# Hybrid decoder block: block 0's mixers first, and both of its expert sums beside the chains

## The chip, the cores and the metric

One core of one Trainium2 chip runs the kernel. The metric is the device time of one execution in microseconds (us); smaller is better. Five engines work side by side, each through its own queue in order: TensorE (PE; its weight loads are shown as PEld), VectorE (DVE), ScalarE (ACT), GpSimd (POOL, which here only issues gathers) and SyncE (SP, which issues all other DMAs).

## The reference

512 tokens of 1024 features go through one decoder layer: two mixers that see earlier tokens (A and B), a merge, and a mixture of single-neuron experts (PEER). Cut to what matters:

```python
h = rms_norm(x, norm1_gain)
proj = h @ w_in                               # column groups for both mixers and both merge gates
# A: per query the indexer picks the 128 best causal keys, attention runs over these alone
score = einsum(iw, relu(iq . ik));  _, sel = top_k(score, k_sel);  y_att = softmax(q . k[sel]) @ v[sel]
# B: gated DeltaNet: short conv, SiLU, per chunk of 64 a triangular solve, a state handed on from chunk to chunk
y_dn = rms_norm(gated_deltanet(...), gain) * silu(dz)
merged = sigmoid(ga) * (y_att @ w_att_branch) + sigmoid(gb) * (y_dn @ w_dn_branch)
x = x + merged @ w_o
h2 = rms_norm(x, norm2_gain)
# PEER: 8 heads, 2 x 128 sub-keys each, top 16 of the sums: 128 experts a token out of 16384
q = h2 @ w_query;  s = q . sub_keys;  top_k, top_k;  expert, gate = ...
act = gelu(sum(u_tab[expert] * h2));  x = x + sum((gate * act) * v_tab[expert])
```

## The kernel before, in words

The tokens are four blocks of 128 (block 0 to block 3). Weights come as tiles of 0.5 MB through four buffers (`wt`). What TensorE makes for block 0 alone reads `h0`, what it makes for the other three blocks at once reads `hr`.

Four *chains* run round robin, each a Python generator that yields between dependent steps: two `deltanet` chains (two heads each, block after block), `indexer` (16 rounds of max and replace on VectorE per block) and `attender`. After each step of a chain a *filler* gets turns, 1.6 per step (`FILL_A`) or 1.8 (`FILL_B`). The filler holds what has no chain: `projections(0)` and `projections(1)` (for block 0 and for the rest), and `single(0)` and `single(1)`, each of which takes one block through merge, `w_o`, second norm, query, sub-keys (`path`) and the choice of its 128 experts (`choose`), and ends with writing the indices `eu` (line 902). In the program before, the filler mixes whatever is active: a block's `single` gets two turns for each one of `projections(1)`.

PEER is done in two ways. Blocks 0 and 1 (`SINGLE`) gather: for each of 128 slots, GpSimd issues one indirect DMA that brings a row of 1024 numbers for each of 128 tokens (0.5 MB, `row`), and VectorE sums it: for a u row a product with `h2` and a sum into `act` (line 923), for a v row a multiple added to `x1` (line 934). That makes 4 x 128 = 512 rows, one after another through `all_rows`: before, u of block 0, u of block 1, v of block 0, v of block 1. The gathers go round four buffers (`ROWS`); late in the program eight more are there (`MORE_ROWS`). Blocks 2 and 3 (`WHOLE`) compute all 16384 experts densely: `dense_u(i)` multiplies with a tile `ut` and takes the gelu into `ge`, `spread` writes the chosen gates into a dense matrix (one-hot `oa`, `ob`, products on TensorE, `gb` to DRAM as `gd`), and `dense_v(i)` multiplies `ge` by the gates and sums with `vt` into `acc`.

The stages follow each other: chains and filler until block 1's indices are there; `path(WHOLE)`, with a row at every second step (`STEPS_E`); 36 `dense_u` around the two `choose`, then 16 chunks of `spread`, with four rows a chunk (`CHUNK_ROWS`) and the rest of the first 54 `dense_u`; then 128 `dense_v` with the other 74 `dense_u` and all rows that are left, paced evenly. A scheduler orders the instructions on every engine from this; each engine then keeps that order.

Of the kernel before, what the change touches and what calls it, by code (L numbers as in the profile page):

```python
# [34 lines left out]

FILL_A = 1.6
FILL_B = 1.8
MORE = 6
# [14 lines left out]
ROWS, MORE_ROWS = 4, 8  # L53
STEPS, STEPS_E, CHUNK_ROWS = 2, 2, 4
END = 3
# [30 lines left out]
def tile_block(ctx, tc, x, xT0, xT1, w_in, sc_cols, sc_rows, w_br, w_o, w_q, subT, uT, uv, cst, iota, out, dbg=None):  # L86
# [17 lines left out]
    def load(dst, src):  # L104
        nc.sync.dma_start(dst, src)
# [134 lines left out]
    done = set()  # L240
    rowv = cp.tile([P, 8 + D], F32, name="rowv")
    load(rowv, sc_rows.to_broadcast([P, 8 + D]))
    alog, dtb, n2g = rowv[:, 0:4], rowv[:, 4:8], rowv[:, 8:8 + D]
    io = cp.tile([P, P], F32, name="io")
# [273 lines left out]
    def projections(part):  # L518
        if part == 0:
            for t in ORDER[6:]:  # L520
                yield from conv(t, 0)
            yield from keys(0)
            yield from queries(0)
            yield from output_gates(0)
            return
        for t in ORDER[:6]:
            yield from conv(t, 1)
        yield from scalars(1)
        for t in ORDER[6:]:
            yield from conv(t, 1)  # L530
        for t in range(4):
            S.copy(iqT[:, t, :], (yield from project(CT_IQ + t, 1)))
            if t == 3:
                done.add("index")
            yield
        yield from output_gates(1)
        yield from keys(1)
        yield from queries(1)
        for t in (8 * br + dt for dt in range(8) for br in range(2)):
            o = yield from project(CT_G + t, 1)  # L540
            s_ = tmp()[:, :T - P]
            S.copy(s_, o)
            nc.sync.dma_start(sgd[t], s_)
            yield
# [187 lines left out]

    x1d = {b: dr.tile([P, D], F32, name=f"x1d{b}") for b in (*SINGLE, *WHOLE)}
    uv2 = uv.rearrange("e (t d) -> (e t) d", t=2)
# [4 lines left out]
    def path(bs, place, banks=("mm",)):  # L739
# [38 lines left out]
        for b in bs:  # L778
            x1[b], h2[b] = place("x1", b), place("h2", b)
            load(x1[b], x[col(b), :])  # L780
        hT_ = place("hT", None)

        def second_norm(b):
            r = slice((b - bs[0]) * P, (b - bs[0] + 1) * P)
            nc.sync.dma_start(x1d[b], x1[b])
            s1 = tiny.tile([P, 1], F32, name="s1", bufs=2)
            r2 = tiny.tile([P, 1], F32, name="r2", bufs=2)
            S.activation(h2[b], x1[b], AF.Square, accum_out=s1)
            V.tensor_scalar(s1, s1, 1.0 / D, EPS, op0=ALU.mult, op1=ALU.add)
            rsqrt(r2, s1, "h")  # L790
            V.scalar_tensor_tensor(h2[b], x1[b], r2, n2g, op0=ALU.mult, op1=ALU.mult)
            for half in range(2):
# [61 lines left out]
    def single(b):  # L854
# [3 lines left out]
        def place(name, _):  # L858
            if name in ("m", "hT"):
                return quarter(name)  # L860
            if name == "x1":
                return hp.tile([P, D], F32, name="x1s", tag="hh", bufs=4)
            if name == "h2":
# [43 lines left out]
    rings = [lambda: ep.tile([P, D], F32, name="row", tag="row", bufs=ROWS)]  # L907
    turn_r, emitted = [0], [0]

# [6 lines left out]
    def all_rows():  # L916

        for b in SINGLE:
            while b not in act:
                yield  # L920
            for s in range(P):
# [3 lines left out]
                yield  # L925
        for b in SINGLE:
            for q in range(4):
# [17 lines left out]
    def fill():  # L945

        active, singles, n, b = [projections(0)], list(SINGLE), 0, None
        nexts = [projections(1)]
        while True:
            if b is None and singles and done >= {("y", singles[0], i) for i in range(3)} and (singles[0] == 0 or not nexts and len(active) == 0):  # L950
                b = singles.pop(0)
                active.append(single(b))
            if nexts and len(active) == 0 or nexts and done >= {("z", 0)}:
                active.insert(0, nexts.pop(0))
            if SINGLE[0] in act and n % STEPS == 0:
                rows()
            n += 1
            for g in active + active[1:]:
                if g not in active:
                    continue  # L960
                try:
                    next(g)
                except StopIteration:
                    active.remove(g)
                    if b in act:
                        b = None
                    continue
                yield
            if not active:
                yield  # L970

# [10 lines left out]
    while chains:  # L982
        turn += 1
        for c in chains + (chains[-1:] if MORE and turn % MORE == 0 else []):
# [3 lines left out]
            try:  # L988
# [3 lines left out]
                continue  # L992
            due += FILL_A if ("attention", 1) not in done else FILL_B
            if hop[0]:
# [13 lines left out]
    hT1 = lp.tile([P, 8, NU], F32, name="hT1")  # L1008
    for b in SINGLE:
        x1[b] = lp.tile([P, D], F32, name=f"x1s{b}")  # L1010
        load(x1[b], x1d[b])
    for b in WHOLE:
        sel[b] = [lp.tile([P, 8, 16], F32, name=f"sel{b}{i}") for i in range(2)]
        gate[b] = lp.tile([P, 8, 16], F32, name=f"gate{b}")
# [105 lines left out]
    for b in WHOLE:  # L1120
# [4 lines left out]
        for _ in spread(b, gp):  # L1125
            n += 1
            dense(left * (NCH - n) // NCH)
            rows(CHUNK_ROWS)
    gx.close()
    rx.close()  # L1130
# [128 lines left out]
```

## Time and profile before

| | |
|---|---|
| median of 3 runs | 1865.47 us (1857.95 to 1873.74) |
| the profiled execution | 1860.58 us |
| its span, from the first to the last instruction | 1858.8 us |
| TensorE busy | 1678.5 us, 90% |
| VectorE busy | 1332.8 us, 72% |
| mean granted TensorE clock | 0.95 |

Busy time is the union of an engine's instructions. "Idle before" names what ended an engine's wait. The span and the waits are of the one profiled execution, which is compared with the median only at the end. A matmul on 32-bit numbers has two records in the trace, a transpose one.

### The profile page before, as it was taken

How to read it: one execution, taken by the hardware profiler on the slowest of the kernel's cores; microseconds unless marked ns; L12 is line 12 of the kernel's file. 1: busy time of each engine (PE TensorE's matmuls, PEld its weight loads, DVE VectorE, ACT ScalarE, POOL GpSimd, SP SyncE). 2: the span in 40 equal slices, each digit the busy share in tenths (PEclk: the TensorE clock that was granted, in tenths of full speed). 3: DMA queues.
4: the chain of work that ended last, by engine and by line, in shares of the span. 5: the costliest groups of instructions: out<-in, count | busy, mean ns of one | idle time of the engine just before them, and what ended most of it. 6: DMA issues, size and time to landing. Idle time of an engine off the chain costs nothing.

```text
span 1858.8 us, 24234 instructions
## 1 busy us (share of the span) xinstructions
PE 1678.5 (90%) x8330; PEld 1311.6 (71%) x8330; DVE 1332.8 (72%) x3114; ACT 573.6 (31%) x1165; POOL 629.4 (34%) x516
## 2 busy tenths in 40 slices
PE   6899999899999968895379997699999999999998
PEld 5766686776667766495269996477777777777766
DVE  3733563978678899789996877886865856567675
ACT  5255322221136314011056885011212222122222
POOL 0000000001542443446834435554533533343430
PEclk8999999999998987997779999799999999999999
DMA  5422355343998899999979999999998999999985
GB/s 212 137 102 74 111 193 195 100 142 106 338 328 319 310 361 336 363 343 360 366 271 343 359 366 389 412 409 409 404 373 325 410 354 365 395 365 362 383 312 170
DMA packets 190123, 556.30 MB, mean 299 GB/s; under 512 B 17840, under 2 KB 63664, under 8 KB 187952
## 3 DMA queue, kind: packets, MB, share of 16 engines
q1 hardware_dynamic: 116272, 286.28, 42.4%
q0 software_dynamic: 73728, 268.47, 38.3%
q8 instruction: 66, 1.08, 0.2%
q14 instruction: 57, 0.47, 0.1%
HBM read 528.60 MB, written 25.95 MB: 298 GB/s over the span
## 4 chain that ended last, share of the span: by engine, by line
PE 54%; DVE 15%; issue 12%; DMA 11%; POOL 5%; ACT 2%; DVEq 0%; POOLq 0%; SPq 0%; ACTq 0%
PE acc L94 18%; PE mm L94 14%; DMA row<-in_uv_dram,eu 9%; PE dn L94 5%; POOL row L913 4%; DVE row L923 3%; PE at L94 3%; DVE wk L573 1%; DVE m L572 1%; DMA row__9423<-in_uv_dram,eu 1%; DMA row__8663<-in_uv_dram,eu 1%; DMA row__7536<-in_uv_dram,eu 0%; DMA row__7605<-in_uv_dram,eu 0%; PE at L609 0%; DMA C<-in_cst_dram 0%
## 5 line engine op out<-in xcount | busy, mean ns | idle before, releaser
L913 POOL DMA_INDIRECT row<-in_uv_dram,eu x318 | 386.3, 1215 | 933.0 <-DVE eu L902 455.3
L923 DVE CUSTOM_DVE_ANT_0 row<-row,h 128x1024 f32<-128x1024 f32 x233 | 281.5, 1217 | 59.4 <-DMA row<-in_uv_dram,eu 58.6
L94 PE MATMUL mm<-hT,ut 128*128 128x256 f32 x864 | 204.5, 394 | 64.4 <-ACT ge L1058 34.2
L94 PE MATMUL mm<-hr,wt 128*128 128x384 f32 (+1 forms) x688 | 241.2, 490 | 0.0
L94 PEld LDWEIGHTS mm<-hT,ut 128*128 128x128 f32 x864 | 168.1, 199 | 89.7 <-ACT ge L1058 35.0
L180 DVE TENSOR_TENSOR vl<-vt,vh 128x1024 fp32r<-128x1024 f32 x86 | 104.0, 1220 | 103.9 <-ACT vh L179 103.8
L94 PEld LDWEIGHTS mm<-hr,wt 128*128 128x128 f32 x688 | 122.9, 190 | 75.9 <-issue 8.6
L94 PE MATMUL acc<-vt,ge 128*128 128x512 f32 x336 | 151.0, 592 | 0.0
L94 PE MATMUL acc<-vl,ch 128*128 128x512 f32 x344 | 139.6, 406 | 6.5 <-DVE vl L180 6.5
L94 PE MATMUL acc<-vh,cl 128*128 128x512 f32 x344 | 135.7, 394 | 0.0
L94 PE MATMUL acc<-vh,ch 128*128 128x512 f32 x344 | 121.9, 437 | 3.8 <-ACT gs L1054 3.8
L179 ACT CAST vh<-vt 128x1024 fp32r<-128x1024 f32 x86 | 88.1, 1044 | 85.7 <-DMA vt<-in_uv_dram 85.1
L934 DVE SCALAR_TENSOR_TENSOR x1s<-row,act,x1s 128x1024 f32<-128x1024 f32 x85 | 109.0, 1282 | 3.0 <-DMA row<-in_uv_dram,eu 1.3
L180 DVE TENSOR_TENSOR cl<-gt,ch 128x256 fp32r<-128x256 f32 x86 | 36.3, 423 | 101.2 <-ACT ch L179 97.9
L94 PEld LDWEIGHTS acc<-vt,ge 128*128 128x128 f32 x336 | 63.8, 190 | 62.6 <-issue 60.3
L179 ACT CAST ch<-gt 128x256 fp32r<-128x256 f32 x86 | 34.7, 404 | 231.9 <-PE acc L94 221.8
L94 PE MATMUL mm<-h,wt 128*128 128x128 f32 x624 | 82.4, 291 | 7.2 <-DVE h L202 4.3
L94 PEld LDWEIGHTS mm<-h,wt 128*128 128x128 f32 x624 | 79.3, 206 | 10.8 <-DVE h L202 4.6
L1098 ACT ACTIVATE ob<-ob,sl 128x128 f32<-128x128 f32 x256 | 78.2, 388 | 26.2 <-DVE ob L1095 26.2
L94 PEld LDWEIGHTS acc<-vh,ch 128*128 128x128 f32 x344 | 66.0, 192 | 26.0 <-issue 8.6
L94 PEld LDWEIGHTS acc<-vl,ch 128*128 128x128 f32 x344 | 65.3, 190 | 22.1 <-DVE vl L180 8.2
L94 PE MATMUL mm<-hT,wt 128*128 128x128 f32 x640 | 79.8, 284 | 1.0 <-ACT tmp L849 1.0
(988 smaller groups left out, 3189.8 us busy)
## 6 DMA issues: line engine op xcount, KB each, us to landing
ut<-in_uT_dram SPq DMA_DIRECT2D x128, 512.0 KB
vt<-in_uv_dram SPq DMA_DIRECT2D x128, 512.0 KB
wt<-in_w_in_dram SPq DMA_DIRECT2D x82, 512.0 KB
wt<-in_w_q_dram SPq DMA_DIRECT2D x48, 512.0 KB
gd<-gb SPq DMA_DIRECT2D x16, 1024.0 KB
gt<-gd SPq DMA_DIRECT2D x16, 1024.0 KB
wt<-in_w_br_dram SPq DMA_DIRECT2D x24, 512.0 KB
wt<-in_w_o_dram SPq DMA_DIRECT2D x24, 512.0 KB
```

The costliest lines, as they stand in the source:

```text
L94: hop[0] = PE.matmul(o, l, r, start=start, stop=stop).ins
L179: S.copy(hi, src)
L180: return V.tensor_tensor(lo, src, hi.bitcast(F32), op=ALU.subtract).ins
L572: V.max(m8, src[:, :N])
L573: V.match_replace(wk[:, :N], m8, src[:, :N], TAKEN)
L913: G.indirect_dma_start(out=r, out_offset=None, in_=uv2, in_offset=bass.IndirectOffsetOnAxis(ap=ix, axis=0))
L923: V.tensor_tensor_reduce(r, r, h2[b], 1.0, 0.0, op0=ALU.mult, op1=ALU.add, accum_out=act[b][:, s:s + 1])
L934: V.scalar_tensor_tensor(x1[b], r, act[b][:, s:s + 1], x1[b], op0=ALU.mult, op1=ALU.add)
L1098: S.activation(ob[:, t], ob[:, t], AF.Copy, scale=sl[:, 2, n:n + 1])
```

## The change

Five things are done at once. The filler's turns are 0.9 per chain step until both halves of block 0's DeltaNet are done (`FILL_0`). The filler no longer mixes: `single(b)` has all turns while it is alive, else the first of the projections. Block 0's v rows come right after its u rows, so before block 1's u rows; its `x1` stays in SBUF for that, and is no longer written to DRAM and read back. Rows come at one per two filler turns from block 0's indices on (`PACE`), at every sixth step of `path(WHOLE)` and two per chunk of `spread`; the number of `dense_u` beside `spread` is kept so that eight stay for its end (`LAST_U`). The second norm's gain is loaded into each `h2` tile instead of once for all, and the square's unused output goes to `hT_`.

```diff
-FILL_A = 1.6
-FILL_B = 1.8
+FILL_0, FILL_A, FILL_B = 0.9, 1.6, 1.8
-STEPS, STEPS_E, CHUNK_ROWS = 2, 2, 4
+PACE, STEPS_E, CHUNK_ROWS = 0.5, 6, 2
+LAST_U = 8
...
-    rowv = cp.tile([P, 8 + D], F32, name="rowv")
-    load(rowv, sc_rows.to_broadcast([P, 8 + D]))
-    alog, dtb, n2g = rowv[:, 0:4], rowv[:, 4:8], rowv[:, 8:8 + D]
+    rowv = cp.tile([P, 8], F32, name="rowv")
+    load(rowv, sc_rows[:, 0:8].to_broadcast([P, 8]))
+    alog, dtb = rowv[:, 0:4], rowv[:, 4:8]
...
-        yield from output_gates(1)
         yield from keys(1)
         yield from queries(1)
+        yield from output_gates(1)
...
             load(x1[b], x[col(b), :])
+            load(h2[b], sc_rows[:, 8:8 + D].to_broadcast([P, D]))
...
-            nc.sync.dma_start(x1d[b], x1[b])
+            if b != SINGLE[0]:
+                nc.sync.dma_start(x1d[b], x1[b])
...
-            S.activation(h2[b], x1[b], AF.Square, accum_out=s1)
+            S.activation(hT_[:, :, r], x1[b].rearrange("p (k c) -> p k c", c=P), AF.Square, accum_out=s1)
...
-            V.scalar_tensor_tensor(h2[b], x1[b], r2, n2g, op0=ALU.mult, op1=ALU.mult)
+            V.scalar_tensor_tensor(h2[b], x1[b], r2, h2[b], op0=ALU.mult, op1=ALU.mult)
...
-        for b in SINGLE:
+            while b and not x1_back:
+                yield
             for q in range(4):
...
-        active, singles, n, b = [projections(0)], list(SINGLE), 0, None
-        nexts = [projections(1)]
+        others, singles, alone, b, due = [projections(0), projections(1)], list(SINGLE), None, None, 0.0
         while True:
...
+            ready = singles and done >= {("y", singles[0], i) for i in range(3)}
+            if alone is None and ready and len(others) <= (singles[0] == 0):
                 b = singles.pop(0)
-                active.append(single(b))
...
-            if SINGLE[0] in act and n % STEPS == 0:
-                rows()
+                alone = single(b)
+            if SINGLE[0] in act:
+                due += PACE
+                while due >= 1.0:
+                    due -= 1.0
+                    rows()
+            if alone is not None:
+                if next(alone, True):
+                    alone = None
+            elif others:
+                if next(others[0], True):
+                    others.pop(0)
+            yield
...
-            due += FILL_A if ("attention", 1) not in done else FILL_B
+            due += FILL_0 if ("y", 0, 0) not in done or ("y", 0, 1) not in done else FILL_A if ("attention", 1) not in done else FILL_B
...
-            dense(left * (NCH - n) // NCH)
+            dense(LAST_U + (left - LAST_U) * (NCH - n) // NCH)
             rows(CHUNK_ROWS)
+    dense(0)
```

Three places show what this moves. The first is TensorE's queue while block 0 goes through its query weights (`mm<-hT,wt`) and sub-keys (`mm<-tmp`). Names that begin with `dn` are DeltaNet's, `at` the indexer's and attention's, and `mm<-hr,wt` are projections of the later blocks. Before:

```order
L94 MATMUL mm<-hT,wt 128x128 x16
L94 MATMUL dn_3231<-XX,am 128x128 x2
L330 MATMUL dn_3284<-C,am 128x128 x2
L94 MATMUL mm<-tmp 128x128 x2
L94 MATMUL dn_3264<-XX,s_3262 128x128 x2
L94 MATMUL dn_3264<-s_3262,XX 128x128 x2
L94 MATMUL mm<-hT,wt 128x128 x10
L94 MATMUL at<-colv,tmp 128x2 x3
L94 MATMUL mm<-hT,wt 128x128 x2
L94 MATMUL at<-ikT,iqT 128x512
L94 MATMUL mm<-hT,wt 128x128 x4
L94 MATMUL mm<-hr,wt 128x384 x8
```

And now:

```order
L96 MATMUL mm<-hT,wt 128x128 x16
L96 MATMUL dn_3320<-kT_3273 128x128 x2
L96 MATMUL mm<-tmp 128x128 x2
L96 MATMUL mm<-hT,wt 128x128 x16
L332 MATMUL dn_3427<-C,am 128x128 x2
L96 MATMUL mm<-tmp 128x128 x2
L96 MATMUL mm<-hT,wt 128x128 x16
L96 MATMUL dn_3484<-XX,am 128x128 x2
L96 MATMUL mm<-tmp 128x128 x2
L96 MATMUL mm<-hr,wt 128x387 x8
```

The projections of the later blocks and most of the chains' steps have moved behind block 0's way. Up to block 0's last sub-key product 1,145 matmuls stand before and 888 now: 200 and 72 with `hr`, 312 and 214 of DeltaNet, 89 and 58 of the indexer, attention and norms, and the same 544 others.

The second place is VectorE's queue behind block 0's indices `eu`. A u row's sum is two instructions, `row,act` and `act`. Before:

```order
L902 SCALAR_TENSOR_TENSOR eu_2991<-area 128x128
L923 ISA row,act_2994<-row,h_0_2093 128x1024
L923 ISA act_2994 128x1
...
L417 TENSOR_TENSOR vb<-dn_3729,beta 128x256
L423 TENSOR_TENSOR attT<-dn_3768,dT 128x256
...
L622 TENSOR_TENSOR tmp<-at,sm 128x2x64
L598 ISA t,mx<-at,bias_1918 128x256
```

And now the place where block 0's u rows end and its v rows begin (`x_0`):

```order
L930 ISA row,act_2247<-row,h_0_1715 128x1024
L930 ISA act_2247 128x1
L939 TENSOR_SCALAR eu_2244<-eu_2244 128x128
L414 TENSOR_TENSOR XX<-XX,dn_4526 64x2x64
L575 MATCH_REPLACE wk<-m_3377,wk 128x384
L423 TENSOR_TENSOR eb<-eb,qhT 128x256
...
L942 SCALAR_TENSOR_TENSOR x_0_1714<-row,act_2247,x_0_1714 128x1024
```

Block 0's v rows now stand among the chains' steps, of which more are left behind `eu0`. `eu0` stands behind 845 other instructions of VectorE before, behind 588 now. `eu1` stands behind 111 u rows and 1,286 other instructions before, and behind 128 u rows, 103 v rows and 1,288 others now. From there to the first product of `dense_v` with the gates stand 171 rows before and 60 now (22 of these 111 ahead of the first `oa`), and behind it 230 and 221.

The third place is VectorE's queue in the middle of `spread`. Before:

```order
L1095 TENSOR_TENSOR oa<-io,sl 128x1024
L1095 TENSOR_TENSOR ob<-io,sl 128x1024
L923 ISA row,act_5191<-row,h_1_4401 128x1024
L923 ISA act_5191 128x1
L923 ISA row,act_5191<-row,h_1_4401 128x1024
L923 ISA act_5191 128x1
L923 ISA row,act_5191<-row,h_1_4401 128x1024
L923 ISA act_5191 128x1
```

And now:

```order
L1098 TENSOR_TENSOR oa<-io,sl 128x1024
L1098 TENSOR_TENSOR ob<-io,sl 128x1024
L1098 TENSOR_TENSOR oa<-io,sl 128x1024
L1098 TENSOR_TENSOR ob<-io,sl 128x1024
L1098 TENSOR_TENSOR oa<-io,sl 128x1024
```

No row stands between the one-hot tiles any more.

## Rows read from the trace of the kernel before

**Rows 1.** The page, part 1: span, then busy time of each engine.

```profile
span 1858.8 us, 24234 instructions
PE 1678.5 (90%) x8330; PEld 1311.6 (71%) x8330; DVE 1332.8 (72%) x3114; ACT 573.6 (31%) x1165; POOL 629.4 (34%) x516
```

**Rows 2.** Line 902: durations in ns, then first and last start.

```profile
L902 DVE SCALAR_TENSOR_TENSOR eu<-area x2: 291/292/293, 455.2 to 750.4; 128x128 int32<-128x128 f32 x2
```

**Rows 3.** The dense end's products, same columns.

```profile
L94 PE MATMUL acc<-vh,ch x344: 387/389/799, 1200.9 to 1851.9; 128*128 128x512 f32 x172
```

**Rows 4.** Windows I to IV: length, busy us, granted clock, DMA share, GB/s.

```profile
0.00:455.50 455.50, 419.64 (x2363) 318.57 (x2364) 270.25 (x966) 157.00 (x316) 0.20 (x4) 0.97 0.39 134
455.50:750.70 295.20, 262.22 (x1381) 197.28 (x1380) 237.80 (x736) 91.95 (x183) 123.76 (x115) 0.91 0.92 331
750.70:1200.90 450.20, 353.76 (x2038) 309.65 (x2037) 378.06 (x902) 181.00 (x423) 236.27 (x187) 0.90 0.97 356
1200.90:1858.80 657.90, 642.87 (x2554) 486.08 (x2552) 446.73 (x512) 143.64 (x243) 269.18 (x212) 0.99 0.94 360
```

**Rows 5.** TensorE's waits in III: us in total, times, longest.

```profile
PE mm L94 <- ACT ge L1058: 34.2, 2, 19.6
PE mm L94 <- DMA ut<-in_uT_dram: 30.2, 4, 18.5
PE at L1083 <- DVE bp L687: 13.2, 1, 13.2
PE at L795 <- DVE r L176: 7.3, 1, 7.3
PE at L1083 <- DVE sel L725: 6.9, 1, 6.9
PE dn L94 <- ACT ob L1098: 3.9, 1, 3.9
PE dn L94 <- ACT qt L842: 0.7, 1, 0.7
```

**Rows 6.** Two short windows of III: PE, PEld, DVE, ACT, POOL, clock, DMA.

```profile
850.00:950.00 100.00, 41.05 (x181) 34.51 (x181) 99.28 (x353) 16.82 (x36) 69.86 (x55) 0.71 0.86 320
1150.00:1175.00 25.00, 6.54 (x22) 5.17 (x21) 9.17 (x8) 2.86 (x4) 6.96 (x7) 0.66 1.04 410
```

**Rows 7.** The chain that ended last, inside II: shares by line.

```profile
by line: DMA row<-in_uv_dram,eu 31.2%; DVE row L923 13.6%; issue 11.0%; PE mm L94 7.6%; PE at L94 5.4%; POOL row L913 5.2%; PE dn L94 4.0%; DVE tmp L776 1.3%; PE at L609 1.3%; ACT L767 1.2%; DMA tmp<-sgd 0.9%; DVE t L598 0.9%; DVE oh_s L721
```

**Rows 8.** Block 0's sub-key matmuls between 400 and 470 us.

```profile
L94 PE MATMUL mm<-tmp x8: 275/275/275, 402.7 to 409.8; 128*128 128x128 f32 x8
```

**Rows 9.** Groups by line: count, busy us, mean ns, idle before.

```profile
L94 PE MATMUL mm<-hr,wt 128*128 128x384 f32 (+1 forms) x688 | 241.2, 490 | 0.0
...
L934 DVE SCALAR_TENSOR_TENSOR x1s<-row,act,x1s 128x1024 f32<-128x1024 f32 x85 | 109.0, 1282 | 3.0 <-DMA row<-in_uv_dram,eu 1.3 <-DVE x1s L934 0.2
...
L94 PE MATMUL dn<-XX,s 128*128 128x128 f32 (+1 forms) x192 | 29.9, 277 | 2.6 <-ACT s L395 1.4 <-ACT s L408 1.2
```

**Rows 10.** Window II, instructions of line 923 alone (two to a row).

```profile
455.50:750.70 295.20, 136.15 (x223) 0.91 0.92 331
```

**Rows 11.** Waits of GpSimd and VectorE in II.

```profile
POOL row L913 <- DVE act L923: 82.6, 47, 5.1
DVE row L923 <- DMA row<-in_uv_dram,eu: 42.6, 36, 5.8
```

**Rows 12.** In order of time, the first gathers: start, duration, idle before.

```profile
455.74 1.07 POOL L913 DMA_INDIRECT row<-in_uv_dram,eu  x1 [455.29 <-DVE eu L902]
457.12 0.94 POOL L913 DMA_INDIRECT row<-in_uv_dram,eu  x1 [0.30 <-issue]
...
461.26 1.22 DVE L923 CUSTOM_DVE_ANT_0 row<-row,h 128x1024 f32<-128x1024 f32 x1 [5.80 <-DMA row<-in_uv_dram,eu]
462.41 0.08 DVE L923 DVE_READ_ACCUMULATOR2_ANT act<- 128x1 f32 x1
```

**Rows 13.** ScalarE's waits between 840 and 960 us.

```profile
ACT act L929 <- DVE act L923: 25.5, 1, 25.5
```

More of the change, by code (lines that the diff above doesn't have):

```diff
@@ L730, in choose @@
             nc.sync.dma_start(dbg["gate"][s, :], g_.rearrange("p h k -> p (h k)"))
-    x1d = {b: dr.tile([P, D], F32, name=f"x1d{b}") for b in (*SINGLE, *WHOLE)}
+    x1d = {b: dr.tile([P, D], F32, name=f"x1d{b}") for b in (*SINGLE[1:], *WHOLE)}
     uv2 = uv.rearrange("e (t d) -> (e t) d", t=2)
@@ L861, in place @@
             if name == "x1":
+                if b == SINGLE[0]:
+                    return ep.tile([P, D], F32, name="x1_0")
                 return hp.tile([P, D], F32, name="x1s", tag="hh", bufs=4)
@@ L907, in tile_block @@
     rings = [lambda: ep.tile([P, D], F32, name="row", tag="row", bufs=ROWS)]
-    turn_r, emitted = [0], [0]
+    turn_r, emitted, x1_back = [0], [0], []
     def row_of(ix):
@@ L945, in fill @@
     def fill():
-        active, singles, n, b = [projections(0)], list(SINGLE), 0, None
-        nexts = [projections(1)]
+        others, singles, alone, b, due = [projections(0), projections(1)], list(SINGLE), None, None, 0.0
         while True:
-            if b is None and singles and done >= {("y", singles[0], i) for i in range(3)} and (singles[0] == 0 or not nexts and len(active) == 0):
+            ready = singles and done >= {("y", singles[0], i) for i in range(3)}
+            if alone is None and ready and len(others) <= (singles[0] == 0):
                 b = singles.pop(0)
-                active.append(single(b))
-            if nexts and len(active) == 0 or nexts and done >= {("z", 0)}:
-                active.insert(0, nexts.pop(0))
-            if SINGLE[0] in act and n % STEPS == 0:
-                rows()
[L957 to L970, printed above, removed]
+                alone = single(b)
[11 more added lines that the diff above has]
+            yield
     sgd = [dr.tile([P, T - P], F32, name=f"sgd{t}") for t in range(16)]
@@ L1008, in tile_block @@
     hT1 = lp.tile([P, 8, NU], F32, name="hT1")
-    for b in SINGLE:
+    for b in SINGLE[1:]:
         x1[b] = lp.tile([P, D], F32, name=f"x1s{b}")
         load(x1[b], x1d[b])
+        x1_back.append(b)
     for b in WHOLE:
```

## The prediction

> **What bounds the kernel now.** I read the totals first [rows 1], and then cut the span at three events that the code names. TensorE is busy 90% of the span, so the time is its work plus the stretches in which it stands still; the question is where those lie, and who makes them. The cuts are the expert indices of block 0 and of block 1 (`eu`, line 902, at 455 and 750 us) [rows 2] and the first product of the dense end (`acc`, at 1200.9 us) [rows 3]. I call the stretches I to IV [rows 4].
>
> In IV TensorE stands for 15 of 657.9 us: nothing but its own work bounds it. In III it stands for 450.2 - 353.8 = 96.4 us, and the list of its waits adds up to just that [rows 5]: 34.2 for gelu buffers, 30.2 for `ut` tiles, 20.1 for the choice (13.2 and 6.9, line 1083), 12 for the rest. VectorE is full there: 99.28 of 100 us between 850 and 950 [rows 6]. In II TensorE stands for 33 us, VectorE for 57. The chain inside II shows what paces it [rows 7]: landing gathers 31.2%, row sums 13.6%, issuing gathers 5.2%. Half of the chain is the loop of a row through its four buffers, although only 111 rows are summed there. So rows are not free beside the chains: that is the point on which I forecast.
>
> **The change, stretch by stretch.** The number of rows, weight tiles and matmuls stays; they move. By the order, 111 row sums stand ahead of `eu1` before and 231 after; between `eu1` and the first gate product 171 before and 60 after; behind it 230 and 221.
>
> *I, to `eu0`.* The last sub-key matmul of block 0 ran at 409.8 us [rows 8]; 1,145 matmuls stood ahead of it. Now 888 do: 128 tiles of the later tokens' projections (`hr`) fewer, at 241.2/344 = 0.70 us each (two records a matmul) [rows 9], 90 us; and 129 small ones of the chains fewer, at 29.9/96 = 0.31 us [rows 9], 40 us. TensorE was busy 419.6 of 455.5 us, so the work taken away is time: 409.8 - 130 = 280. The choice took 455.2 - 409.8 = 45 us beside other VectorE work, of which less is left: 40. `eu0` comes at **320**, 135 us sooner.
>
> *II, `eu0` to `eu1`.* Up to `eu1` VectorE did 270.3 + 237.8 = 508.1 us of work [rows 4], of which rows 136.2 [rows 10], 1.23 each: 371.9 of other work, by 1,286 instructions. Now 588 of these stand ahead of `eu0`, at the mean 170 us; 202 us are left for II. To these come 128 row sums of u at 1.23 (157 us) and, new here, 103 of v at 1.28 (132 us) [rows 9]. That is **491 us of VectorE work in one queue, in order, against 237.8 before**. No cover exists for it: `eu1`'s own choice stands behind the rows in that queue. To the work come waits. VectorE stood 42.6 us for gathers over 111 rows [rows 11], 0.38 a row, and 15 us for all else. The upper bound is 231 x 0.38 + 15 = 104 us. The lower is one filling of the ring, 5.8 us [rows 12], if all other gathers come in time behind other work. Rows stand 2.1 us apart in the order on average (491/231), a little closer than they ran in II (295.2/111 = 2.7), and a gather takes 455.74 to 461.26, or 5.5 us, before a buffer can be summed [rows 12], so with 1.3 for its sum and 0.3 until the next issue four buffers give a row every 1.8 us at best. That lies close to the spacing, so I stay nearer the upper end: 65. II lasts 556 and `eu1` comes at **876**, 125 us later than now. TensorE has 419.6 + 262.2 - 290 = 392 us of work for these 556; it will stand for some 160, and its granted clock, 0.91 in II, will fall further, which costs nothing while VectorE is last. DMA moved 331 GB/s in II, 97.7 MB; 120 more rows of 0.52 MB and 16 more weight tiles make 169 MB, 304 GB/s over 556 us: it is not the tighter bound, but it forbids less than 169/356 = 475 us at the rate of III.
>
> *III.* 111 rows leave, 111 x 1.23 = 137 us of VectorE's 378.1. TensorE's 353.8 us stay. Of its waits, one gelu wait of 19.6 us goes for sure: ScalarE stood at block 0's own gelu (line 929), 25.5 us for the last row of u [rows 13], and that is now in II. The `ut` waits, the longest 18.5 us at 1150 to 1175, where DMA ran at 410 GB/s [rows 6], go with the rows beside the spread; the eight `dense_u` kept for its end fill what the landing gates leave open. The choice stays: it is a chain on VectorE, but with 22 rows less ahead of it (27 us) it costs perhaps 12 of its 20. Bounds for what is left: 12 us (the rest alone) and 76 (only the sure one gone); I take 30, since VectorE's relief is larger than all waits together. III lasts **384**, 66 us less.
>
> *IV.* 221 instead of 230 rows, under TensorE's work: 658, as now.
>
> *The small edits.* Four loads of the norm's gain, 0.5 MB each, replace one; the write and reading back of block 0's `x1` go (1 MB). That is some 0.5 MB more, on SP's queue beside 169 MB: nothing. The square's output goes to another tile, at the same size: nothing. Reordered projections (output gates last) move no work.
>
> Sum: 320 + 556 + 384 + 658 = 1918, and the 1.8 us that lie around the span (1860.6 - 1858.8): **1920**. The profiled execution took 1860.6, 4.9 under the median of 1865.5; I compare with the former for the sum. A measurement of this kernel can tell about 1% from no change.
>
> **A rule that speaks against the change.** A gather's issue lasted 123.76/115 = 1.08 us in II, and 69.86/55 = 1.27 where VectorE was full [rows 4, 6]. This agrees with the Trainium skill, "SBUF — State Buffer", section "SBUF: two separate sides": GpSimd writes the descriptors of its DMAs through a port that some VectorE instructions lock, so a full VectorE starves gathers. By the rule each turn of the four-slot ring is 0.19 us longer, 231/4 turns, 11 us, and the sum 1931.
>
> **Rivals.**
> *Faster: the rows slip in between.* If gathers nearly always land behind other VectorE work, II costs 491 + 5 and III keeps 12 us of waits: 315 + 496 + 366 + 658 + 2 = **1837**. For it speaks that VectorE ran at 99.28% among rows from 850 on [rows 6]; against it that eight more buffers stood there, and that II waited for 36 gathers with more room between them [rows 11]. It decides where VectorE's idle time in II and TensorE's in III together stay under some 25 us. The Trainium skill, "DMA: Bandwidth & Descriptors", section "Anatomy of one DMA — SWDGE (gpsimd) path", gives 2.0 us and the bytes at 436 GB/s, by which an estimate for a gather is 3.2 us and this rival would hold; the trace's 5.5 us disagrees.
> *About even: half of it.* Waits of 20 in II and 20 in III: 320 + 511 + 374 + 658 + 2 = **1865**.
> *Slower still: each row waits as now, and III is not freed.* 104 in II and 76 in III: 320 + 595 + 430 + 658 + 2 = **2005**; half of that excess, 1960, is what I think possible.
> *It doesn't do what it says.* If the scheduler kept rows between the spread's steps, III would keep its `ut` waits: 25 us more, 1945. The order shows no row there, so I give it little.
>
> **How the numbers follow.** The forecast has 0.55 with its neighbours from 1884 to 1950; the faster rival 0.13 (all below 1847); the even case 0.17 (1847 to 1884); the two slow ones 0.15. Likeliest 1920. The range leaves out the faster rival's core and the far slow end: 1858 to 1972. Faster by over 1%: 0.13; within: 0.17; slower: 0.70.
>
> **What the profile after would show.** `eu0` near 320 and the first gather right behind it: if it comes past 350, step I is wrong. `eu1` near 876, with VectorE busy about 490 us between the two and TensorE at some 70%: if `eu1` stands before 830, the waits for rows were overrated, and the result is even or faster. The stretch from `eu1` to the first `acc` near 384, with `ut` waits gone. The dense end within 10 us of 658. The prediction falls if II is short because VectorE's other work lies elsewhere than the order's mean says, or if III's waits were not VectorE's doing.

## The result, and the profile after

The changed kernel takes 1928.31 us (median of 4 runs, 1920.08 to 1935.84), the kernel before 1868.86 beside it: a ratio of 1.0326, 95% interval 1.0258 to 1.0393. It is slower, by 8 us more than the 1920 that was forecast. Its profiled execution took 1924.78 us, of which the span is 1923.0.

The page, part 1, and the events at which the span is cut, of the changed kernel; they answer to [rows 1 to 3, 8]:

```profile
span 1923.0 us, 24217 instructions
PE 1707.5 (89%) x8330; PEld 1320.9 (69%) x8330; DVE 1323.2 (69%) x3114; ACT 566.1 (29%) x1160; POOL 605.3 (31%) x516
...
L96 PE MATMUL mm<-tmp x32: 275/275/377, 252.4 to 286.3; 128*128 128x128 f32 x32
...
L909 DVE SCALAR_TENSOR_TENSOR eu<-area x2: 291/293/295, 317.2 to 860.3; 128x128 int32<-128x128 f32 x2
...
L96 PE MATMUL acc<-vh,ch x344: 387/393/799, 1272.4 to 1916.2; 128*128 128x512 f32 x172
```

Windows I to IV of the changed kernel, columns as in [rows 4]:

```profile
0.00:317.50 317.50, 285.33 (x1805) 235.62 (x1806) 168.92 (x663) 116.28 (x234) 0.20 (x4) 0.96 0.49 166
317.50:860.60 543.10, 428.41 (x1942) 295.75 (x1942) 477.92 (x1180) 126.97 (x261) 252.02 (x234) 0.86 0.89 313
860.60:1272.40 411.80, 361.90 (x2097) 318.39 (x2095) 234.54 (x655) 178.18 (x422) 78.29 (x69) 0.95 0.74 254
1272.40:1923.00 650.60, 631.90 (x2488) 471.13 (x2488) 441.81 (x620) 144.69 (x244) 274.83 (x209) 0.99 0.92 353
```

Beside [rows 4], I is 138 us shorter, II 247.9 longer, III 38.4 and IV 7.3 shorter: 64.2 us in all. The work on VectorE is the same (1323 against 1333 us). TensorE is busy 29 us longer with as many matmuls (its granted clock in II is 0.86 beside 0.91), and stands 215.5 us instead of 180.3.

VectorE's waits in II, which answer to [rows 11], then TensorE's in II, then TensorE's in III, which answer to [rows 5]:

```profile
DVE row L930 <- DMA row<-in_uv_dram,eu: 33.5, 38, 2.8
DVE x L942 <- DMA row<-in_uv_dram,eu: 23.8, 24, 2.8
...
PE dn L332 <- DVE ot L459: 41.0, 2, 37.3
PE dn L96 <- DVE XX L401: 12.0, 10, 2.9
PE at L96 <- ACT R L563: 11.5, 1, 11.5
...
PE mm L96 <- ACT ge L1061: 19.5, 2, 18.8
PE at L1086 <- DVE sel L727: 11.9, 2, 6.9
PE at L800 <- DVE rs_t L177: 5.5, 1, 5.5
```

Waits for gathers in II are 57 us; with 8 us for all else they make the 65 that were forecast. In III the `ut` waits [rows 5] are down to 0.7 us, and a gelu wait of 18.8 us stays. New is a stand of TensorE for one DeltaNet step, 37.3 us long. It is the thread that the experiments follow.

### The profile page after: what moved, and what is told of

Read it like the earlier page. It is cut to its first block, busy times and chain, and to the rows that moved or that the text cites. A ratio compares the mean times of both kernels' runs of the same rounds, so it can differ in the third digit from the quotient of the medians.

```text
span 1923.0 us, 24217 instructions
## 1 busy us (share of the span) xinstructions
PE 1707.5 (89%) x8330; PEld 1320.9 (69%) x8330; DVE 1323.2 (69%) x3114; ACT 566.1 (29%) x1160; POOL 605.3 (31%) x516
## 3 DMA queue, kind: packets, MB, share of 16 engines
q8 instruction: 66, 1.08, 0.2%
## 4 chain that ended last, share of the span: by engine, by line
PE 38%; DVE 9%; issue 9%; DMA 7%; POOL 4%; ACT 1%; SPq 0%; DVEq 0%; POOLq 0%; ACTq 0%
PE acc L96 11%; PE mm L96 11%; PE dn L96 5%; DMA row<-in_uv_dram,eu 3%; POOL row L920 2%; PE at L96 2%; DVE x L942 1%; DMA gt<-gd 1%; DMA wt<-in_w_br_dram 1%; DVE row L930 1%; DMA ut<-in_uT_dram 1%; DVE ti L657 0%; DMA gd<-gb 0%; DVE sr L655 0%; DVE ti L654 0%
## 5 line engine op out<-in xcount | busy, mean ns | idle before, releaser
L96 PE MATMUL mm<-hr,wt 128*128 128x384 f32 (+1 forms) x688 | 248.6, 506 | 0.5 <-issue 0.5
L930 DVE CUSTOM_DVE_ANT_0 row<-row,h 128x1024 f32<-128x1024 f32 x173 | 210.5, 1219 | 33.9 <-DMA row<-in_uv_dram,eu 33.5
L96 PE MATMUL mm<-hT,ut 128*128 128x256 f32 x864 | 198.9, 387 | 23.3 <-ACT ge L1061 19.5
L96 PEld LDWEIGHTS mm<-hr,wt 128*128 128x128 f32 x688 | 128.0, 196 | 92.7 <-issue 24.3
L942 DVE SCALAR_TENSOR_TENSOR x<-row,act,x 128x1024 f32<-128x1024 f32 x128 | 163.7, 1279 | 34.8 <-DMA row<-in_uv_dram,eu 34.0
L1098 DVE TENSOR_TENSOR oa<-io,sl 128x1024 f32<-128x1024 f32 x32 | 39.1, 1223 | 138.2 <-PE dn L96 138.2
L96 PE MATMUL acc<-vh,ch 128*128 128x512 f32 x344 | 115.5, 434 | 7.2 <-ACT ch L181 5.3
L182 DVE TENSOR_TENSOR cl<-gt,ch 128x256 fp32r<-128x256 f32 x86 | 36.3, 423 | 105.9 <-ACT ch L181 103.3
```

The lines of the kernel that those rows point to most:

```text
L96: hop[0] = PE.matmul(o, l, r, start=start, stop=stop).ins
L182: return V.tensor_tensor(lo, src, hi.bitcast(F32), op=ALU.subtract).ins
L930: V.tensor_tensor_reduce(r, r, h2[b], 1.0, 0.0, op0=ALU.mult, op1=ALU.add, accum_out=act[b][:, s:s + 1])
L942: V.scalar_tensor_tensor(x1[b], r, act[b][:, s:s + 1], x1[b], op0=ALU.mult, op1=ALU.add)
L1098: V.tensor_tensor(o_, io[:, None].to_broadcast([P, TB, P]), which, op=ALU.is_equal)
```

## The experiments

The first table gives what each kernel is; rows are counted in the order of VectorE's queue ahead of `eu1`, from there to the first gate product, and behind it. Stages are those of the profiled execution, in us, cut to within 0.4. Medians are of the timed runs; the three kernels without an interval had one execution each.

| kernel | rows | I | II | III | IV | median, ratio [95%] |
|---|---|---|---|---|---|---|
| before | 111, 171, 230 | 455.5 | 295.2 | 450.2 | 657.9 | 1863 to 1869 |
| changed | 231, 60, 221 | 317.5 | 543.1 | 411.8 | 650.6 | 1928.31, 1.033 [1.026, 1.039] |
| half row pace | 142, 32, 338 | 319.2 | 478.1 | 432.2 | 774.3 | 2001.27, 1.074 [1.071, 1.077] |
| half row pace, 6 a chunk | 142, 96, 274 | 317.5 | 479.9 | 456.6 | 691.0 | 1940.68, 1.042 [1.040, 1.044] |
| narrow gather | 249, 42, 221 | 320.3 | 518.0 | 378.9 | 627.6 | 1846.62 |
| routing as before | 231, 141, 140 | 319.7 | 545.0 | 446.7 | 640.4 | 1953.5, 1.049 [1.047, 1.051] |
| turns alone | 222, 63, 227 | 320.1 | 530.4 | 444.0 | 664.6 | 1962.02, 1.054 [1.050, 1.059] |
| turns undone | 110, 153, 249 | 453.9 | 286.7 | 443.4 | 679.7 | 1870.68, 1.005 [1.002, 1.007] |
| even pace | 144, 147, 221 | 393.8 | 364.5 | 433.3 | 649.0 | 1841.57, 0.988 [0.984, 0.993] |
| before, new routing | 111, 94, 307 | 457.4 | 296.5 | 440.7 | 725.3 | 1912.03, 1.026 [1.021, 1.030] |
| pace 1.25 | 222, 70, 220 | 346.7 | 521.0 | 428.3 | 655.1 | 1953.44, 1.047 [1.043, 1.051] |
| pace alone | 128, 163, 221 | 355.4 | 444.5 | 455.6 | 667.3 | 1932.88, 1.036 [1.033, 1.040] |
| no early rows, 0.9 | 36, 21, 455 | 318.3 | 364.8 | 435.4 | 906.2 | 2026.44 |
| no early rows, 1.6 | 36, 21, 455 | 393.6 | 301.9 | 428.1 | 907.3 | 2032.72 |

### Are the rows late by their transfer, or by VectorE's queue?

The narrow gather fetches 64 columns a row, and the sum reads them 16 times, so that VectorE's work is the same and the bytes are a sixteenth; the experts' values are left out.

```diff
-    rings = [lambda: ep.tile([P, D], F32, name="row", tag="row", bufs=ROWS)]
+    rings = [lambda: ep.tile([P, 64], F32, name="row", tag="row", bufs=ROWS)]
...
-                V.tensor_tensor_reduce(r, r, h2[b], 1.0, 0.0, op0=ALU.mult, op1=ALU.add, accum_out=act[b][:, s:s + 1])
+                V.tensor_tensor_reduce(in16(junk), wide(r), in16(h2[b]), 1.0, 0.0, op0=ALU.mult, op1=ALU.add, accum_out=act[b][:, s:s + 1])
```

> The changed kernel, but each gather brings 64 columns in place of 1024, from other places of the table, and the sums run over 1024 columns by reading these 64 sixteen times; it leaves out the values of the experts, the numbers of instructions stay. 249 rows stand ahead of eu1. Theory (VectorE's queue): VectorE's work in II is 189 + 249 x 1.25 = 500 us, its waits for rows go, II lasts about 508 us. Rival (the ring of gathers and DMA's rate pace II): II falls to TensorE's 428 us and little more, about 440.

Window II of the narrow gather, columns as above:

```profile
320.30:838.30 518.00, 438.75 (x1988) 298.95 (x1987) 495.44 (x1204) 130.44 (x264) 298.08 (x252) 0.88 0.37 114
```

II fell by 25 us only, with DMA at 114 GB/s instead of 313: VectorE is busy 495 of 518 us. The transfers are not what makes II long; 18 more rows slipped into it. The ring and the DMA as the cause fall.

### Fewer rows ahead of the second indices

Two kernels: half the row pace with the changed kernel's two rows a chunk of `spread`, and with six.

```diff
-PACE, STEPS_E, CHUNK_ROWS = 0.5, 6, 2
+PACE, STEPS_E, CHUNK_ROWS = 0.25, 6, 2
...
-PACE, STEPS_E, CHUNK_ROWS = 0.5, 6, 2
+PACE, STEPS_E, CHUNK_ROWS = 0.25, 6, 6
```

> The changed kernel with PACE 0.25 in place of 0.5: by the order 142 rows stand ahead of eu1 (231 in the changed kernel), 32 between eu1 and the first gate product, 338 behind it. Theory (II is VectorE's queue, its rows and its waits for them): VectorE's work in II falls to 189 + 142 x 1.25 = 367 us, TensorE's 428 us is last, II falls from 543 to about 470 and eu1 comes near 787. III stays near 405. The rows go into IV, which moves 230 MB in 651 us; 117 more rows make 291 MB, at 405 GB/s 719 us, so IV becomes 720 and the whole 1914. Rival (the turns' order, which leaves the later blocks' projections and chains for II, and not the rows, makes II long): II stays over 520, the whole near 1970. Second rival (IV has room under TensorE's work): IV stays at 655, the whole near 1850.

> The changed kernel with PACE 0.25 and six rows a chunk of the spread in place of two: 142 rows ahead of eu1, 96 up to the first gate product, 274 behind it. Theory: II 470 as with half the pace, III 425 (VectorE 314 of it), IV 655 (258 MB), the whole 1869, as the kernel before. Rival (turns' order): II over 520, the whole 1920 or more.

Both took far longer than expected: II missed by 8 to 10 us, but IV took 774.3 instead of 720 and 691.0 instead of 655, and with six rows a chunk III took 456.6 instead of 425.

89 rows fewer ahead of `eu1` bring it 63 us forward, 0.7 us a row, where a row's sum alone is 1.22 to 1.28. And `eu1` comes at 797 with 142 rows ahead of it, where before it came at 750 with 111. VectorE was busy 369 of II's 478 us, so its queue was not full; TensorE stood 36.3 us for the same `ot`. That was the first sign that something besides the number of rows costs. The other finding is in IV: 338 rows there made 774.3 us. TensorE's wait in IV, of the half row pace:

```profile
PE acc L96 <- DVE vl L182: 93.3, 19, 10.5
```

The dense end needs VectorE for splitting its weights (`vl`), and row sums stand ahead of these. By the table, IV takes 640 us with 140 rows, 649 to 667 with 220 to 230, 680 with 249, 691 with 274, 725 with 307, 774 with 338 and 906 with 455: up to some 220 rows cost little, beyond that about 1.1 us each on the mean ((906.2 - 650.6)/234, from the changed kernel to no early rows at 0.9).

### The routing part

The changed kernel with the old routing, and the old kernel with the new routing (`STEPS_E`, `CHUNK_ROWS`, `LAST_U`).

```diff
-PACE, STEPS_E, CHUNK_ROWS = 0.5, 6, 2
+PACE, STEPS_E, CHUNK_ROWS = 0.5, 2, 4
...
-            dense(LAST_U + (left - LAST_U) * (NCH - n) // NCH)
+            dense(left * (NCH - n) // NCH)
```

And in the kernel before:

```diff
-STEPS, STEPS_E, CHUNK_ROWS = 2, 2, 4
+STEPS, STEPS_E, CHUNK_ROWS = 2, 6, 2
+LAST_U = 8
...
-            dense(left * (NCH - n) // NCH)
+            dense(LAST_U + (left - LAST_U) * (NCH - n) // NCH)
...
+    dense(0)
```

> The changed kernel with the routing part undone (a row at every second step of the path, four rows a chunk, no dense_u kept for the end): I and II stay as in the changed kernel, 317 and 543 us. Theory (rows beside the routing delay what TensorE waits for): 81 rows more in III, 100 us of VectorE's time, III goes from 412 to about 440 us; IV, bound by TensorE, stays at 645 with 140 rows; the whole is 1947, 1% over the changed kernel. Rival (III is bound by TensorE's work, rows there are free): III stays at 415 and the whole at 1920.

> The kernel before with the routing part of the change alone: a row at every sixth step of the last blocks' path, two a chunk of spread, eight dense products kept for its end. Rows 111 ahead of the second indices, 94 from there to the first gate product, 307 behind. Indices as before (455, 750). If rows beside the routing are what stretches it, the third stage falls from 450 to 400 or so, and the dense end, by the runs with 274 (691) and 338 rows (774) in it, rises from 658 to 730: 1885. If the waits there were not VectorE's doing, the third stage stays at 450 and the whole takes 1930.

In the changed kernel the new routing is worth 35 us of III and gives 10 back in IV, near what was expected. In the old kernel it saves 9.5 us of III and costs 67 in IV, because 307 rows are left for it: 1912.03 instead of the 1885 expected. So in these two kernels fewer rows beside the routing pay only where the rows were summed before it.

### Turns, pace of turns, or rows?

Three kernels undo one part of the change each. *Turns alone* keeps the turns and emits as many rows at each stage as the old kernel, with its routing:

```diff
-PACE, STEPS_E, CHUNK_ROWS = 0.5, 6, 2
+PACE, STEPS_E, CHUNK_ROWS = 0.316, 2, 4
...
-            dense(LAST_U + (left - LAST_U) * (NCH - n) // NCH)
+            dense(left * (NCH - n) // NCH)
```

*Turns undone* has the old mixing filler, the old order of projections and 1.6 turns, with the new order of rows and as many of them emitted at each stage as in the changed kernel:

```diff
-FILL_0, FILL_A, FILL_B = 0.9, 1.6, 1.8
+FILL_0, FILL_A, FILL_B = 1.6, 1.6, 1.8
-PACE, STEPS_E, CHUNK_ROWS = 0.5, 6, 2
+PACE, STEPS_E, CHUNK_ROWS = .79, 6, 2
...
-                alone = single(b)
+                active.append(single(b))
...
-            if alone is not None:
-                if next(alone, True):
-                    alone = None
...
+            for g in active + active[1:]:
```

*Even pace* undoes `FILL_0` alone, with a row pace that keeps the count of emitted rows:

```diff
-FILL_0, FILL_A, FILL_B = 0.9, 1.6, 1.8
+FILL_0, FILL_A, FILL_B = 1.6, 1.6, 1.8
-PACE, STEPS_E, CHUNK_ROWS = 0.5, 6, 2
+PACE, STEPS_E, CHUNK_ROWS = 0.655, 6, 2
```

> The changed kernel's turns, chain pace and order of row sums, but as many rows at each stage as before: PACE 0.316, a row at every second step of the last blocks' path, four a chunk of spread, no dense products kept for its end. 285 rows stand ahead of the first gate product (before 282, changed 291), 227 behind. If the cost is the rows' work in VectorE's queue, this kernel has no more of it than the one before: first gate product near 1205, dense end 655, 1865 in all. If the order of turns itself costs (at half the pace the gate product came at 1229 with only 174 rows ahead of it, 28 us later than before with 282), it comes at 1290 to 1310, and the whole takes 1945 to 1965.

> The changed kernel with the old mixing filler, the old pace of turns (1.6) and the old order of projections, but the new row order (block 0's v behind its u), the new routing and a row pace that emits as many rows as the changed kernel at each stage (233, 258 and 290 by the end of chains, path and spread). The scheduler sets 110 rows ahead of the second indices, 153 from there to the first gate product, 249 behind. If the order of turns is what costs, this is as fast as the kernel before or faster: 750 to the second indices, gate product 1175 to 1200, dense end 665, 1845 to 1865. If the row order and row pace cost, the gate product comes near 1270 as in the changed kernel, and the whole takes 1930.

> The changed kernel with 1.6 turns per chain step from the start (FILL_0 undone) and PACE 0.655, so that again 234, 259 and 291 rows are emitted by the end of chains, path and spread. By the order 778 other instructions of VectorE stand ahead of the first indices instead of 588, 144 rows ahead of the second ones, 147 from there to the first gate product, 221 behind. If the loss lies in the chains' being hurried first and TensorE's later standing idle for them, block 0's indices come at 390 to 420, the gate product at 1210 to 1230, the whole takes 1870 to 1890. If it lies in the filler's turns by block alone or in the rows, it stays at 1920 to 1935.

Turns alone is slower than the changed kernel, with the old kernel's count of rows ahead of the gate products (285 against 282). Turns undone equals the kernel before within half a per cent (1870.68 us, a little over the 1845 to 1865 that were expected). And the even pace, with all else of the change but its row pace, is faster than the kernels before and after: 1841.57 us, 0.988 of the kernel before, and faster than the 1870 to 1890 that were expected. It comes to the gate products at 1191.6 us where the changed kernel comes at 1272.4, with 291 rows ahead of them in both. Its windows:

```profile
0.00:393.80 393.80, 365.57 (x2199) 287.34 (x2200) 241.97 (x883) 140.43 (x291) 0.20 (x4) 0.98 0.42 145
393.80:758.30 364.50, 321.88 (x1533) 233.79 (x1532) 302.00 (x870) 101.72 (x204) 157.49 (x147) 0.88 0.91 327
758.30:1191.60 433.30, 355.18 (x2050) 311.35 (x2048) 351.28 (x767) 178.39 (x418) 204.24 (x163) 0.90 0.96 345
1191.60:1840.60 649.00, 637.99 (x2554) 481.69 (x2552) 432.22 (x600) 145.27 (x247) 257.66 (x203) 1.00 0.92 356
```

I loses 76 us to the changed kernel and II wins 179 back. But the scheduler also sets 144 rows ahead of `eu1` here, not 231, and in the other two 222 and 110, so the pace and the rows ahead of `eu1` had to be told apart.

### The pace by itself, with rows and without

*Pace alone* is the kernel before with `FILL_0 = 0.9` and nothing else:

```diff
-            due += FILL_A if ("attention", 1) not in done else FILL_B
+            due += FILL_0 if ("y", 0, 0) not in done or ("y", 0, 1) not in done else FILL_A if ("attention", 1) not in done else FILL_B
```

*Pace 1.25* stands between 0.9 and 1.6, and the two kernels without early rows have `PACE` 0, one at 0.9 turns, one at 1.6:

```diff
-FILL_0, FILL_A, FILL_B = 0.9, 1.6, 1.8
+FILL_0, FILL_A, FILL_B = 1.25, 1.6, 1.8
-PACE, STEPS_E, CHUNK_ROWS = 0.5, 6, 2
+PACE, STEPS_E, CHUNK_ROWS = 0.56, 6, 2
...
-PACE, STEPS_E, CHUNK_ROWS = 0.5, 6, 2
+PACE, STEPS_E, CHUNK_ROWS = 0.0, 6, 2
```

> The kernel before with one edit, 0.9 turns per chain step until both halves of block 0's DeltaNet are done. By the order 626 other instructions of VectorE stand ahead of the first indices (before 846), 128 rows ahead of the second ones (111), 163 from there to the gate product (171), 221 behind (230). If rows ahead of the second indices make the loss, it is 17 rows, some 20 to 25 us: second indices near 773, 1885 in all. If the hurried chains make it by themselves, some 40 us come on top: second indices at 790 to 815, gate product 1240 to 1260, 1915 to 1930.

> The changed kernel with 1.25 turns per chain step at first, half way between its 0.9 and the even 1.6, and PACE 0.56, so that again 292 rows stand ahead of the first gate product. The scheduler sets 663 other instructions of VectorE ahead of the first indices, and 222 rows ahead of the second ones: nearly as many as in the changed kernel (231), where the even pace has 144. If the rows ahead of the second indices make the loss, these come at 840 to 860, the gate product at 1255 to 1275, and the whole takes 1910 to 1925. If the hurried chains themselves make it, half of the difference goes: second indices near 805, gate product near 1230, 1880 in all.

> The changed kernel with PACE 0: no row before the last blocks' path, so 455 rows fall into the dense end and the total time means nothing; 36 rows stand ahead of the second indices by the order. It prices the hurried chains without rows, by the time of the second indices, against its twin at 1.6 turns. If only rows cost, the second indices come in both within 10 us of each other, at 700 to 720, where TensorE's own work (675 to 690 up to there) ends. If the hurried chains cost by themselves, they come 30 to 45 us later here than there.

> The twin of the run without early rows, with 1.6 turns per chain step from the start: 36 rows ahead of the second indices. Second indices at 700 to 720 in either theory; what counts is the difference to the twin. Beside the run at the same pace with 144 rows ahead of the second indices (758), it also gives what such rows cost there: 40 to 58 us for 108 rows if some of them slip into VectorE's idle time, 160 if each costs its full 1.25 us and its wait.

The single edit of the pace makes the old kernel 3.6% slower, as slow as the whole change, with only 17 more rows ahead of `eu1`. In that kernel the number of rows there is not the cause, then. Nor is the hurry by itself: without early rows `eu1` comes at 683 us at 0.9 turns and at 695 at 1.6 (one execution each), so that the hurry gains 12, where a loss of 30 to 45 was expected if it cost by itself. Only both together lose. Rows ahead of `eu1` cost 63 us for 108 at 1.6 turns (695 to 758) and 114 us for 106 at 0.9 (683 to 797): with nearly the same rows ahead of it, `eu1` comes 39 us later at the hurried pace. VectorE's waits in II show where these 39 us are, first of the half row pace (142 rows, 0.9 turns), with its window, then of the even pace (144 rows, 1.6 turns):

```profile
319.20:797.30 478.10, 388.71 (x1824) 267.34 (x1823) 369.29 (x1077) 125.92 (x258) 158.25 (x147) 0.87 0.73 250
DVE row L930 <- DMA row<-in_uv_dram,eu: 39.4, 42, 3.2
DVE t L600 <- PE at L96: 13.1, 10, 3.4
DVE lists L653 <- ACT tmp L854: 12.4, 6, 4.0
```

```profile
DVE row L930 <- DMA row<-in_uv_dram,eu: 43.9, 38, 4.7
DVE XX L401 <- PE dn L96: 3.8, 3, 1.5
DVE t L600 <- PE at L96: 3.6, 4, 1.2
```

Waits for gathers are alike in the two, 43 and 45 us. But VectorE stands 66 us for all else, nearly all of it TensorE's and ScalarE's results, at the half row pace, and 17 at the even pace. With 128 rows and 0.9 turns (pace alone) it stands about 60 us for all else. With 231 rows (the changed kernel) it stands 8: its queue is full, and nothing that TensorE is late with holds it up.

Pace 1.25 points the same way. It has 222 rows ahead of `eu1`, which comes at 867 us, no earlier than in the changed kernel (860). It was expected at 840 to 860 if rows ahead of `eu1` cost, and near 805 if the hurry does; so for kernels with that many rows this run speaks for the rows. It took 1953 us in all, where 1910 to 1925 and 1880 were expected; why it is slower than the changed kernel stays open. No kernel here has 1.6 turns and some 230 rows ahead of `eu1`.

Where rows and hurry meet is seen in windows of 50 us (TensorE's busy time is the second number), of the changed kernel, then without early rows at 0.9, then at the even pace:

```profile
400.00:450.00 50.00, 26.36 (x138) 18.22 (x138) 45.11 (x116) 7.37 (x17) 27.98 (x25) 0.80 0.84 286
450.00:500.00 50.00, 22.77 (x62) 12.26 (x63) 43.36 (x124) 9.24 (x21) 28.94 (x26) 0.62 0.81 275
```

```profile
400.00:450.00 50.00, 49.24 (x192) 28.98 (x191) 24.02 (x79) 13.32 (x32) 0.00 (x0) 1.00 0.30 96
450.00:500.00 50.00, 50.00 (x180) 28.36 (x178) 34.14 (x107) 12.77 (x29) 0.00 (x0) 1.00 0.29 92
```

```profile
400.00:450.00 50.00, 42.43 (x179) 28.94 (x177) 43.48 (x99) 8.37 (x20) 27.25 (x23) 0.86 0.85 293
450.00:500.00 50.00, 48.04 (x164) 28.40 (x165) 44.39 (x127) 12.76 (x30) 22.86 (x23) 0.93 0.93 329
```

VectorE is as busy at the changed and at the even pace (88 us), and the gathers nearly (57 and 50 us of issuing); TensorE does 49 us of work in the one and 90 in the other. The timeline of the changed kernel in that hole: first TensorE, then VectorE's queue meanwhile (start, duration, idle before in brackets).

```profile
430.17 0.39 PE L96 MATMUL dn<-vn,attT 128*128 128x128 f32 x2
467.81 0.66 PE L332 MATMUL dn<-C,ot 128*128 128x128 f32 x2 [37.25 <-DVE ot L459]
...
438.07 1.21 DVE L930 CUSTOM_DVE_ANT_0 row<-row,h 128x1024 f32<-128x1024 f32 x1
439.21 0.08 DVE L930 DVE_READ_ACCUMULATOR2_ANT act<- 128x1 f32 x1
439.21 0.16 DVE L173 TENSOR_SCALAR rs_t<-s 128x2 int32<-128x2 int32 x1
440.03 1.22 DVE L930 CUSTOM_DVE_ANT_0 row<-row,h 128x1024 f32<-128x1024 f32 x1 [0.66 <-DMA row<-in_uv_dram,eu]
441.18 0.08 DVE L930 DVE_READ_ACCUMULATOR2_ANT act<- 128x1 f32 x1
441.18 0.16 DVE L173 TENSOR_SCALAR rs_t<-s 128x2 int32<-128x2 int32 x1
441.25 0.42 DVE L574 MAX8 m<-wk 128x8 f32<-128x256 f32 x1
441.59 0.15 DVE L174 TENSOR_SCALAR r<-rs_t 128x2 int32<-128x2 int32 x1
```

The norm of a DeltaNet output is a chain of small steps on 2 numbers a partition (`rs_t`, `r`, `rs_a`), 0.15 us each, and ahead of nearly every one stands a row sum of 1.22 us, with the wait for its gather. The norm's first and last steps (ScalarE's square of `ot`, VectorE's product `ot`; minimum, median and maximum in ns, then first and last start) of the changed kernel, without early rows at 0.9, and at the even pace:

```profile
L339 ACT ACTIVATE s<-ot x2: 417/417/417, 429.7 to 431.0; 128x256 f32<-128x256 f32 x2
L459 DVE TENSOR_TENSOR ot<-ot,r x2: 420/445/470, 467.2 to 467.6; 128x256 f32<-128x256 f32 x2
```

```profile
L339 ACT ACTIVATE s<-ot x1: 417/417/417, 465.5 to 465.5; 128x256 f32<-128x256 f32 x1
L459 DVE TENSOR_TENSOR ot<-ot,r x1: 408/408/408, 475.3 to 475.3; 128x256 f32<-128x256 f32 x1
```

```profile
L339 ACT ACTIVATE s<-ot x2: 416/416/417, 444.5 to 448.9; 128x256 f32<-128x256 f32 x2
L459 DVE TENSOR_TENSOR ot<-ot,r x2: 406/412/418, 483.5 to 486.9; 128x256 f32<-128x256 f32 x2
```

Without rows the norm takes 9.8 us; with rows it takes 37 at the hurried pace, and 38 to 39 at the even one as well. The even pace pays next to nothing for it, because of what TensorE's queue holds between (its groups from 449 to 487 us at the even pace):

```profile
L96 PE MATMUL mm<-hr,wt 128*128 128x384 f32 x80 | 30.1, 527 | 0.0
```

Eighty records, or forty products, of the later blocks' projections stand between the output and its transposes, and TensorE is busy 35.0 of these 38 us. In the changed kernel none stands there: the transposes follow the output directly, and everything behind them waits, projections too. That these products make the difference is read from the two traces; no run moves them alone. The half row pace has the same stand (36.3 us). In pace alone TensorE stands 26.3 us at the same place, right behind the output, but for a step of the indexer (`R`), for which ScalarE in its turn waited 24.9 us for VectorE.

## Why the prediction came out, point by point

The sum is nearer than its terms. The four stretches missed by -2.5, -13, +28 and -7 us, which leave 5; so close a sum is luck.

**I** was forecast at 320 and took 317.5. The last sub-key product came at 286.3, not 280, and the choice behind it took 31 us, not 40. The prediction gives the whole gain to what no longer stands ahead in TensorE's queue, and does not say which edit makes it: of the 138 us, the even pace has 62 with 1.6 turns, and the 0.9 turns bring the other 76.

**II** was forecast at 556 and took 543.1, with 478 us of VectorE work (491 forecast) and 57 us of waits for gathers and 8 of others (65 forecast). TensorE stood 115 us, not 160. The terms are right in size, and the waits stayed nearer the upper end, as chosen. The narrow gather confirms that VectorE, not the transfers, paced the rows. For this kernel the mechanism holds too: VectorE works or waits for a row in 535 of the 543 us, so that TensorE's standing, the 37.3 us included, "costs nothing while VectorE is last". What the prediction did not see is what lies under it. With fewer rows ahead of `eu1`, VectorE is no longer last, and at 0.9 turns TensorE's stands then come back to it as waits: pace alone is as slow with 128 rows and VectorE busy 340 of 444.5 us. What the rows do there is stretch the chain's small steps nearly four times over; what that costs depends on whether TensorE's queue holds other work at those places, and `FILL_0` took it away. So `FILL_0` gains 76 us in I, and it alone makes the old kernel 3.6% slower. With 1.6 turns and a row pace to match, the rest of the change is 1.2% faster than the kernel before. How the changed kernel's own loss divides between its 231 rows ahead of `eu1` and the 0.9 turns is not shown.

**III** was forecast at 384 and took 411.8; this is the term that was mis-sized. TensorE's work was 361.9 instead of 353.8 us, and its waits were 49.9 instead of 30. The `ut` waits and 8 of the choice's 20 us went as forecast; a gelu wait such as the one that was to go "for sure" was there again. It stands at 981 to 1000 us, and ScalarE was then waiting 22.6 us for VectorE's gates of the choice, with the gelus queued behind:

```profile
ACT gate L692 <- DVE gate L691: 22.6, 1, 22.6
...
999.96 5.26 PE L96 MATMUL mm<-hT,ut 128*128 128x256 f32 x16 [18.79 <-ACT ge L1061]
```

**IV** was forecast at 658 and took 650.6, with 221 rows; the table's slope beyond 221 rows shows that this stage was near its edge.

The **rival that it doesn't do what it says** is out: no row stands between the spread's steps, and the `ut` waits are down to 0.7 us. The **faster rival**, that gathers nearly always land behind other work, is out too: VectorE waited 57 us for them, not 5. So is the **even case**, with 20 us of waits in II and 20 in III: they were 65 and 50. The **slower rival**, each row at its upper price, did not occur.

The **rule on the shared port** (the Trainium skill, "SBUF — State Buffer", section "SBUF: two separate sides") would make a gather's issue longer where VectorE holds the port, by the prediction where VectorE is full. From stage to stage the issue does not follow VectorE's share: in II of the changed kernel VectorE was busy 88%, and an issue took 252.02/234 = 1.08 us, as in II before; in IV, with VectorE at 68%, it took 274.83/209 = 1.31. So the 11 us did not appear. Within a stage the trace agrees with the rule's direction: in II the 25 issues during which VectorE was idle for over half of the time took 0.95 us on the mean and the other 209 took 1.09; in IV 29 took 0.98 and 180 took 1.37. What makes the rest of the difference between the stages stays open.

## What to carry to other kernels

Work that is put "beside" a chain of small dependent steps on the same in-order engine stretches every link by its own length: 1.2-us sums between 0.15-us steps made a 10-us norm last 38. Ask then first whether that engine is full: if it is, each piece of work costs its own length, as here with 231 rows. If it is not, ask what the engine that waits for the chain's end has in its queue meanwhile: with independent products spread over the whole chain TensorE worked 35 of the same 38 us, and with the chain hurried ahead of them it stood for 37. A stage that is bound by one engine takes another engine's extra work for nothing only up to a point, which a few runs find: here some 220 rows under the dense end, and about 1.1 us for each one more.

## What the runs showed of the hardware

TensorE's granted clock fell while it stood: over the 37 us in which it did nothing it was 0.53, close to the lower of its two levels (1.2 of 2.4 GHz). The first products behind the stand (`dn<-C,ot`, 128x128) took 421 to 448 ns each, where the same products took 273 without early rows, at a granted clock of 1.00. So a stand costs TensorE more than its own length. TensorE's busy time ahead of the gate products is 1075.6 us in the changed kernel and 1042.6 at the even pace, and the 33 us between them come on top of 47.8 us more standing. Four more `dense_u` stand ahead of the gate products there, 14 us together; in the other 19 us as many products take longer. That this is the clock is likely, but no run separates it from other causes.
